# Projections with stationary weights in a four-layer hybrid model: the two halves of the activations side by side under one weight

## The chip, the cores and the metric

The kernel runs on one core of one Trainium2 chip. The metric is the device time of one execution, in microseconds (us), lower is better. Three runs of the kernel before took 2116.32, 2118.42 and 2120.05 us; their median, 2118.42, is the time before.

## What is computed

Four layers on h of 256 tokens by 2048 features, float32 throughout, each followed by a residual and a layer norm. Cut to what the change touches, the projections:

```python
def ssd_mixer(h, ...):                       # layer 0
    z, xbc, dt = split(h @ w_in, [4096, 4096 + 6144])
    xbc = silu(causal_depthwise_conv(xbc, conv_w, conv_b))
    dt = softplus(dt + dt_bias)              # 64 heads
    ...                                      # chunked scan, y
    return (rms_norm_by_group(y * silu(z)) * norm_w) @ w_out
def fox_mixer(h, ...):                       # layer 1
    q, k, v, z, f = split(h @ w_in, ...)     # 16 heads of 128
    cum = cumsum(log_sigmoid(f + f_bias))    # added to the logits
    return (causal_attention(q, k, v, cum) * silu(z)) @ w_out
def mla_mixer(h, ...):                       # layer 2
    q_lat, kv_lat, k_pe, z = split(h @ w_in, ...)
    ...
    return (o * silu(z)) @ w_out
def s5_mixer(h, ...):                        # layer 3
    u, z = split(h @ w_in, 2)
    ...                                      # a scan over time: y
    y = gelu(y)
    y = y * sigmoid(y @ w_glu + b_glu)
    return (y * silu(z)) @ w_out
for i in range(4):
    h = layer_norm(8 ** 0.25 * h + mixer[i](h, ...))
```

## The kernel before

**Every product is three matmuls.** A float32 operand is split in two of type fp32r: a high part (a cast) and a low part (the operand less the cast). `mm3` (L110) issues high weights by high activations (L113), then two cross products (L114, L115), all added in PSUM; low by low is left out. The weights arrive in float32: `half` (L91) loads half a strip, 512 KB, by a DMA that SP issues into `raw` (7 buffers); ACT casts it to `whi` (L102) and VectorE (DVE) subtracts to give `wlo` (L107; 4 buffers each; a share goes to GpSimd, POOL). The activations h are kept transposed, features on partitions: `new_hT` and the layer's end (`out_layer`) write them as 16 blocks `hh` (high) and 16 blocks `hl` (low) of 128x256, four blocks to a tile.

**Three shapes of projection** use them:

- `proj_tok` (PSUM tiles `pt`): the activations are the stationary operand (128x128), 512 columns of weights stream past. SSD's z, all output projections, FoX's v and S5's u are made so.
- `proj_Tk` (`pk`): part of MLA.
- `proj_T` (L134, through `proj_T_steps`, L123): the weights are the stationary operand, and the 256 tokens of hT stream past. One call makes one tile of 128 features by 256 tokens, from 16 blocks (kb) of three matmuls with 256 columns each, in half a bank of PSUM. There are 146 such tiles: 48 of SSD's convolution (`cps`, L471) and one of dt (`dps`); 16 each of FoX's q, k and z (`fox_q`, `fox_k`, `zps`) and one of f (`fps`); 16 of MLA's z, 16 of S5's z (`zps`) and 16 of S5's gate (`gps`). That is 2304 blocks in the 144 wide ones. ACT and DVE read the finished tile from PSUM, several times for most: in SSD ACT scales it and DVE adds three shifted products of it.

**The order.** The program names the work in a written order; `defer(n, f)` puts a piece off by n ticks, and a tick passes with each half strip that a projection uses up. Pieces that wait for another engine are put off so. The scheduler of the language then fixes the order on each engine; each engine works its own row of instructions off in that order and waits where an operand is not there.

**SSD**, eight groups: z (`pt`), then `decay` (POOL broadcasts rows across partitions, L514; DVE subtracts; ACT exponentiates), six convolution tiles, and by ticks `turn_x` (transposes `xp`), `inputs` (POOL scales `xdd` and `xs`, L565), `within` (`yd`; POOL's `gate`, L570), `across` (L595, and the second gate), and `turn_y` (transposes `ypt`, L613, of the `xs` that ACT scaled in L601). So POOL goes from broadcasts to two-input operations and back several times a group.

**FoX**, sixteen heads: `fox_q`, `fox_k`, ACT's copies of both to SBUF (L697), then by ticks the logits (`lps`, L704 and L706; DVE scales and masks them, L708 and L710), the softmax, and `zps`. Between the heads run pieces of S5's parameters (`s5_params`): a transpose `wp` (L1036), POOL's operations `wn` (L1101) to `pn` (L1108), and the store of `pn` from an earlier round, `P_d` (L1053), which ACT's queue issues, so ACT stands at it until `pn` is written.

**S5**: `z_tile` is called between the pieces of the scan; `far` are the matmuls that read the scan's state X. After `gelu`, `gps` tiles use a block order of their own.

Of the kernel before, what the change touches and what calls it, by code (L numbers as in the profile page):

```python
# [19 lines left out]
P = 128  # L20
T = 256
# [9 lines left out]
class Core:  # L31
# [59 lines left out]
    def half(self, src, i, n=2048, spare=None):  # L91
# [6 lines left out]
        if spare:  # L98
            hi, lo = (pool.tile([P, n // 2], F32R, tag=t, bufs=b, name=f"w_{t}") for pool, t, b in spare)
        else:  # L100
            hi, lo = (self.wp.tile([P, n // 2], F32R, tag=t, bufs=4, name=t) for t in ("whi", "wlo"))
# [21 lines left out]
    def proj_T_steps(self, src, hT, ps, m=P, order=range(KB)):  # L123

        for i in range(2):
            w = self.half(src, i, KB * m)
            for j in range(8):
                kb = 8 * i + j
                self.mm3(ps, [x[:, j * m:(j + 1) * m] for x in w], [x[order[kb]] for x in hT], kb == 0, kb == KB - 1)
                if j == 7:  # L130
                    self.tick()
                yield

    def proj_T(self, src, hT, ps, m=P, order=range(KB)):  # L134
        for _ in self.proj_T_steps(src, hT, ps, m, order):
            pass

    def proj_tok(self, srcs, aT, n=512, before=None, tail=None, spare=None):
# [10 lines left out]
        while h < N:  # L149
# [9 lines left out]
            for r, (i, t) in enumerate(runs):  # L159
# [4 lines left out]
                for j in range(2):  # L164
                    for tt in range(2) if t is None else (t,):
                        kb = 2 * (h + i) + j
                        a = [x[kb][:, tt * P:(tt + 1) * P] for x in aT]
# [8 lines left out]
    def proj_Tk(self, srcs, aT):  # L176
# [4 lines left out]
        for q, src in enumerate(srcs):  # L181
            for i in range(2):
                w = self.half(src, i)
                for j in range(2):
                    kb = 4 * q + 2 * i + j
                    a = [x[kb] for x in aT]
# [86 lines left out]
    def out_layer(self, li, parts, gb_tiles, spare, out=None):  # L273
# [10 lines left out]
        hT = ([None] * KB, [None] * KB)  # L284
# [38 lines left out]
        def turn(t, k0, nk):  # L323
            c = k0 // 4
            if t == 0 and k0 % 4 == 0:
                for i, n in enumerate("hl"):
                    x = self.hp.tile([P, 4, T], F32R, tag=f"h{n}{c}", name=f"h{n}{c}")
                    hT[i][4 * c:4 * c + 4] = [x[:, k] for k in range(4)]
                    tiles[i].append(x)
# [4 lines left out]
            hi, lo = (x[c][:, k0 % 4:k0 % 4 + nk, t * P:(t + 1) * P] for x in tiles)  # L334
# [3 lines left out]
        tiles = ([], [])  # L338
# [93 lines left out]
def ssd(C, hT, out):  # L432
# [3 lines left out]
    with C.tc.tile_pool(name="ssd", bufs=1) as sp, C.tc.tile_pool(name="ssd_c", bufs=1) as vp, C.tc.tile_pool(name="ssd_t", bufs=1) as tp:  # L436
# [45 lines left out]
        def decays():  # L482
            dps = C.acc("dps")
            C.proj_T(A["ssd_dt"], hT, dps[0:NH, 0:T], m=NH)
            x = arena[0:NH, 0:T]
            nc.vector.tensor_scalar(x, dps[0:NH, 0:T], dtb, None, op0=ALU.add)
# [137 lines left out]
        for g in range(G):  # L624
# [3 lines left out]
                           [[(C.hp, f"h{n}{c}", 1) for n in "hl"] for c in range(4)], out)  # L628


def fox(C, hT, out):
# [3 lines left out]
    with pool(name="fox", bufs=1) as fp, pool(name="fox_t", bufs=2) as tp, \  # L635
# [13 lines left out]
        fps = C.acc("fps")  # L649
        C.proj_T(A["fox_f"], hT, fps[0:H, 0:T], m=H)  # L650
        x, lf, one = V[2][0:H, 0, 0:T], V[2][0:H, 0, T:], V[2][0:H, 1, 0:T]
        nc.vector.tensor_scalar(x, fps[0:H, 0:T], fb, None, op0=ALU.add)
# [33 lines left out]
        def head(h):  # L686
# [6 lines left out]
            for nm in ("fox_q", "fox_k"):  # L693
                ps = C.acc(nm)
                C.proj_T(A[nm][h], hT, ps[:, 0:T])
                s = tp.tile([P, T], F32, tag=nm, name=nm)
                nc.scalar.copy(s, ps[:, 0:T])  # L697
# [29 lines left out]
            nc.scalar.activation(th, zps[:, 0:T], AF.Tanh, scale=0.5)  # L727
            nc.vector.scalar_tensor_tensor(th, th, 1.0, zps[:, 0:T], op0=ALU.add, op1=ALU.mult)
# [4 lines left out]
        for _ in steps:  # L733
# [3 lines left out]
                           [[(C.hp, f"h{n}{c}", 1) for n in "hl"] for c in range(4)], out)  # L737
# [20 lines left out]
def mla(C, hT, out):  # L758
# [3 lines left out]
    with C.tc.tile_pool(name="mla", bufs=1) as mp, C.tc.tile_pool(name="mla_w", bufs=1) as wp, C.tc.tile_pool(name="mla_t", bufs=2) as tp:  # L762
# [84 lines left out]
        for h in range(H):  # L847
            zps = C.acc("zps")
            C.proj_T(A["mla_z"][h], hT, zps[:, 0:T])
            th = tp.tile([P, T], F32, tag="th", name="th")  # L850
            nc.scalar.activation(th, zps[:, 0:T], AF.Tanh, scale=0.5)
# [653 lines left out]
```

## Time and profile before

| what | value |
|---|---|
| median of 3 runs | 2118.42 us |
| the profiled execution as a whole | 2125.38 us |
| its span, to which all rows refer | 2123.2 us |
| mean clock granted to TensorE | 0.979 of full |
| matmuls in the profile | 14409 |
| read from HBM | 357.81 MB, 175 GB/s with the writes |
| weight casts L102 | 611, 630.3 us of ACT |
| low parts L107 | 610, 763.9 us of DVE |

How to read the rows that the prediction quotes. A row of the timeline is: time from the start of the span, duration, engine, line, operation, output<-inputs, shape, count; in brackets the idle time ahead of it and what ended it ("issue": nothing that the profile shows). A row of the stretches is: from:to and its length, then for each of PE, PEld, DVE, ACT and POOL the busy time with the number of instructions, the granted clock, the mean busy share of the DMA engines and GB/s. The sum and mean row is over all stretches asked for. A row of the waits is: who waits at which line <- whom it waits for, with the sum of the waiting in us, how often, and the longest. A group's row gives the engine, the line, the operation and its tiles, with count and durations in ns (lowest, middle, highest, or busy time and mean). PE is TensorE, PEld its weight load.

### The profile page before, as it was taken

How to read it: one execution, taken by the hardware profiler on the slowest of the kernel's cores; microseconds unless marked ns; L12 is line 12 of the kernel's file. 1: busy time of each engine (PE TensorE's matmuls, PEld its weight loads, DVE VectorE, ACT ScalarE, POOL GpSimd, SP SyncE). 2: the span in 40 equal slices, each digit the busy share in tenths (PEclk: the TensorE clock that was granted, in tenths of full speed). 3: DMA queues.
4: the chain of work that ended last, by engine and by line, in shares of the span. 5: the costliest groups of instructions: out<-in, count | busy, mean ns of one | idle time of the engine just before them, and what ended most of it. 6: DMA issues, size and time to landing. Idle time of an engine off the chain costs nothing.

```text
span 2123.2 us, 36603 instructions
## 1 busy us (share of the span) xinstructions
PE 2030.1 (96%) x14409; PEld 1839.9 (87%) x14409; DVE 1377.3 (65%) x2390; ACT 952.9 (45%) x1434; POOL 393.2 (19%) x477
## 2 busy tenths in 40 slices
PE   8999999999999997899999999999999998989997
PEld 7889988998878876799999978998887898989985
DVE  7777677777754694465655567646556776976655
ACT  5455544455443432344444444545544344345442
POOL 0221222122200017778770000000000000000003
PEclk9999999999999998999999999999999999989999
DMA  8445444544576545565666564654347555576662
GB/s 285 152 150 174 157 140 155 170 149 154 164 233 188 185 141 168 172 205 179 220 186 211 178 207 128 205 181 143 106 149 218 179 178 164 169 222 216 190 188 92
DMA packets 131436, 374.30 MB, mean 176 GB/s; under 512 B 33648, under 2 KB 38208, under 8 KB 130496
## 3 DMA queue, kind: packets, MB, share of 16 engines
q1 hardware_dynamic: 108832, 362.07, 54.1%
q10 hardware_dynamic: 21408, 9.83, 1.6%
q8 instruction: 113, 1.85, 0.4%
q14 instruction: 59, 0.48, 0.1%
q0 software_dynamic: 1024, 0.07, 0.0%
HBM read 357.81 MB, written 14.04 MB: 175 GB/s over the span
## 4 chain that ended last, share of the span: by engine, by line
PE 77%; DVE 11%; DMA 5%; POOL 3%; issue 3%; ACT 2%; SPq 0%; ACTq 0%; DVEq 0%; POOLq 0%
PE pt L115 10%; PE pt L113 10%; PE pt L114 10%; PE cps L115 4%; PE cps L114 4%; PE cps L113 4%; PE zps L113 3%; PE zps L114 3%; PE zps L115 3%; DVE wlo L107 3%; PE fox_q L113 1%; PE gps L113 1%; PE gps L114 1%; PE gps L115 1%; PE fox_k L113 1%
## 5 line engine op out<-in xcount | busy, mean ns | idle before, releaser
L107 DVE TENSOR_TENSOR wlo<-raw,whi 128x1024 fp32r<-128x1024 f32 (+3 forms) x610 | 763.9, 1256 | 510.8 <-ACT whi L102 499.4
L102 ACT CAST whi<-raw 128x1024 fp32r<-128x1024 f32 (+3 forms) x611 | 630.3, 1036 | 834.9 <-PE pt L115 306.5
L113 PE MATMUL pt<-whi,hh 128*128 128x512 f32 (+2 forms) x716 | 283.0, 396 | 17.9 <-ACT whi L102 17.6
L114 PE MATMUL pt<-wlo,hh 128*128 128x512 f32 (+2 forms) x716 | 280.0, 391 | 5.8 <-DVE wlo L107 3.1
L115 PE MATMUL pt<-whi,hl 128*128 128x512 f32 (+2 forms) x716 | 280.8, 392 | 0.4 <-DVE hl L336 0.4
L113 PE MATMUL zps<-hh,whi 128*128 128x256 f32 x768 | 223.3, 291 | 0.0
L115 PE MATMUL zps<-hh,wlo 128*128 128x256 f32 x768 | 220.5, 287 | 0.3 <-DVE wlo L107 0.3
L114 PE MATMUL zps<-hl,whi 128*128 128x256 f32 x768 | 220.5, 287 | 0.0
L114 PE MATMUL cps<-hl,whi 128*128 128x256 f32 x768 | 217.8, 284 | 0.0
L115 PE MATMUL cps<-hh,wlo 128*128 128x256 f32 x768 | 217.8, 284 | 0.0
L113 PE MATMUL cps<-hh,whi 128*128 128x256 f32 x768 | 217.7, 283 | 0.0
L113 PEld LDWEIGHTS pt<-whi,hh 128*128 128x128 f32 x716 | 136.9, 191 | 46.5 <-ACT whi L102 18.4
L114 PEld LDWEIGHTS pt<-wlo,hh 128*128 128x128 f32 x716 | 137.0, 191 | 34.8 <-DVE wlo L107 5.4
L115 PEld LDWEIGHTS pt<-whi,hl 128*128 128x128 f32 x716 | 137.1, 191 | 27.1 <-issue 1.7
L113 PEld LDWEIGHTS zps<-hh,whi 128*128 128x128 f32 x768 | 150.5, 196 | 0.5
L115 PEld LDWEIGHTS zps<-hh,wlo 128*128 128x128 f32 x768 | 150.4, 196 | 0.5 <-DVE wlo L107 0.5
L114 PEld LDWEIGHTS zps<-hl,whi 128*128 128x128 f32 x768 | 150.5, 196 | 0.0
L114 PEld LDWEIGHTS cps<-hl,whi 128*128 128x128 f32 x768 | 147.5, 192 | 0.3
L113 PEld LDWEIGHTS cps<-hh,whi 128*128 128x128 f32 x768 | 147.5, 192 | 0.3
L115 PEld LDWEIGHTS cps<-hh,wlo 128*128 128x128 f32 x768 | 147.5, 192 | 0.1
L113 PE MATMUL pt<-whi,yh 128*128 128x512 f32 x240 | 95.6, 398 | 0.0
L114 PE MATMUL pt<-wlo,yh 128*128 128x512 f32 x240 | 95.5, 398 | 0.0
(503 smaller groups left out, 4253.5 us busy)
## 6 DMA issues: line engine op xcount, KB each, us to landing
raw<-in_ssd_z SPq DMA_DIRECT2D x64, 512.0 KB
raw<-in_ssd_x SPq DMA_DIRECT2D x64, 512.0 KB
raw<-in_ssd_o SPq DMA_DIRECT2D x64, 512.0 KB
raw<-in_fox_v SPq DMA_DIRECT2D x32, 512.0 KB
raw<-in_fox_q SPq DMA_DIRECT2D x32, 512.0 KB
raw<-in_fox_k SPq DMA_DIRECT2D x32, 512.0 KB
raw<-in_fox_z SPq DMA_DIRECT2D x32, 512.0 KB
raw<-in_fox_o SPq DMA_DIRECT2D x32, 512.0 KB
```

Source lines behind the costliest of these rows:

```text
L102: nc.scalar.copy(hi, r)
L107: (nc.gpsimd if on_pool else nc.vector).tensor_tensor(lo, r, hi, op=ALU.subtract)
L113: mm(ps, s[0], m[0], start=first, stop=False)
L114: mm(ps, s[0], m[1], start=False, stop=False)
L115: mm(ps, s[1], m[0], start=False, stop=last)
```

## The change

The high and the low activations of a block come to lie in one tile, `[128, 2, 4, 256]`, so that one access pattern takes both: hT gets a third list, the pair. In `proj_T_steps` a block is now two matmuls, the high weights by the pair (512 columns: high in the tile's first half, low in its second) and the low weights by the high activations (256 columns, added to the first half). A tile of output now fills a bank of PSUM, `[m, 2, 256]`, and the sum of its halves is made by `total`: ACT copies the second half to SBUF, and DVE adds the first to it. Everything behind reads the sum from SBUF. In FoX the copies of q and k were there before; the additions are new. Elsewhere copy and addition are both new, with a new tile `u` in SSD and `z` in FoX.

`proj_tok` and `proj_Tk` take the first two lists and issue what they did. S5's tiles `ux` and `un` become one joint tile `xu` (its gelu output too), and the lists of spare weight buffers name the joint tiles.

```diff
 def half(self, src, i, n=2048, spare=None):
...
+                both = pool.tile([P, 2, n // 2], F32R, tag=t, bufs=b, name=f"w_{t}")
+                hi, lo = both[:, 0], both[:, 1]
...
 def proj_T_steps(self, src, hT, ps, m=P, order=range(KB)):
+        mm = self.nc.tensor.matmul
         for i in range(2):
             w = self.half(src, i, KB * m)
             for j in range(8):
                 kb = 8 * i + j
-                self.mm3(ps, [x[:, j * m:(j + 1) * m] for x in w], [x[order[kb]] for x in hT], kb == 0, kb == KB - 1)
+                hi, lo = (x[:, j * m:(j + 1) * m] for x in w)
+                mm(ps, hi, hT[2][order[kb]], start=kb == 0, stop=False)
+                mm(ps[:, 0], lo, hT[0][order[kb]], start=False, stop=kb == KB - 1)
...
-    def proj_T(self, src, hT, ps, m=P, order=range(KB)):
-        for _ in self.proj_T_steps(src, hT, ps, m, order):
+    def proj_T(self, src, hT, name, m=P):
+        ps = self.acc(name)[0:m].rearrange("p (n t) -> p n t", n=2)
+        for _ in self.proj_T_steps(src, hT, ps, m):
             pass
+        return ps
+
+    def total(self, out, ps):
+        self.nc.scalar.copy(out, ps[:, 1])
+        self.nc.vector.tensor_tensor(out, ps[:, 0], out, op=ALU.add)
...
     def new_hT(self):
-        tiles = [[self.hp.tile([P, 4, T], F32R, tag=f"h{n}{c}", name=f"h{n}{c}") for c in range(4)] for n in "hl"]
-        return tuple([x[k // 4][:, k % 4] for k in range(KB)] for x in tiles)
+        tiles = [self.hp.tile([P, 2, 4, T], F32R, tag=f"h{c}", name=f"h{c}") for c in range(4)]
+        return tuple([tiles[k // 4][:, i, k % 4] for k in range(KB)] for i in (0, 1, slice(0, 2)))
...
         def conv(src, ti, pool_tag, bufs):
-            ps = C.acc("cps")
-            C.proj_T(src, hT, ps[:, 0:T])
+            ps = C.proj_T(src, hT, "cps")
+            u = vp.tile([P, T], F32, tag="u", name="u", bufs=2)
+            C.total(u, ps)
             c = vp.tile([P, T], F32, tag="conv", name="conv", bufs=2)
-            nc.scalar.activation(c, ps[:, 0:T], AF.Identity, bias=cb[:, ti:ti + 1], scale=cw[:, ti, 3:4])
+            nc.scalar.activation(c, u, AF.Identity, bias=cb[:, ti:ti + 1], scale=cw[:, ti, 3:4])
             for k in range(1, 4):
-                nc.vector.scalar_tensor_tensor(c[:, k:], ps[:, 0:T - k], cw[:, ti, 3 - k:4 - k], c[:, k:], op0=ALU.mult, op1=ALU.add)
+                nc.vector.scalar_tensor_tensor(c[:, k:], u[:, 0:T - k], cw[:, ti, 3 - k:4 - k], c[:, k:], op0=ALU.mult, op1=ALU.add)
...
             for nm in ("fox_q", "fox_k"):
-                ps = C.acc(nm)
-                C.proj_T(A[nm][h], hT, ps[:, 0:T])
+                ps = C.proj_T(A[nm][h], hT, nm)
                 s = tp.tile([P, T], F32, tag=nm, name=nm)
-                nc.scalar.copy(s, ps[:, 0:T])
+                C.total(s, ps)
                 qk.append(s)
...
-            zps = C.acc("zps")
-            C.proj_T(A["fox_z"][h], hT, zps[:, 0:T])
+            zps = C.proj_T(A["fox_z"][h], hT, "zps")
+            z = tp.tile([P, T], F32, tag="z", name="z", bufs=1)
+            C.total(z, zps)
...
         def z_tile(kb):
-            zps = C.acc("zps")
-            C.proj_T(A["s5_z"][kb], hT, zps[:, 0:T])
+            C.total(zs[kb], C.proj_T(A["s5_z"][kb], hT, "zps"))
...
         for kb in range(KB):
-            gps = C.acc("gps")
-            C.proj_T(A["s5_glu"][kb], (yh, yl), gps[:, 0:T], order=order)
+            gps = C.acc("gps").rearrange("p (n t) -> p n t", n=2)
+            for _ in C.proj_T_steps(A["s5_glu"][kb], (yh, yl, yb), gps, order=order):
+                pass
             s = tp.tile([P, T], F32, tag="th", name="sg", bufs=3)
-            nc.scalar.activation(s, gps[:, 0:T], AF.Tanh, bias=bg[:, kb:kb + 1], scale=0.5)
+            C.total(s, gps)
+            nc.scalar.activation(s, s, AF.Tanh, bias=bg[:, kb:kb + 1], scale=0.5)
```

The change also moves instructions. In FoX, DVE's row of one head before, from the first low part of a weight half to the two logits operations:

```order
L107 TENSOR_TENSOR wlo<-raw,whi 128x1024
L271 TENSOR_TENSOR y_9665<-yf,y_9664 128x256
L107 TENSOR_TENSOR wlo<-raw,whi 128x1024 x2
L708 SCALAR_TENSOR_TENSOR lg<-lps,ckm 128x256
L710 SCALAR_TENSOR_TENSOR lg<-lps,ck 128x128
```

and the same place now (L153 is the addition in `total`, L112 the low part):

```order
L153 TENSOR_TENSOR fox_q<-fox_q 128x256
L112 TENSOR_TENSOR wlo<-raw,whi 128x1024
L288 TENSOR_TENSOR y_8770<-yf,y_8769 128x256
L112 TENSOR_TENSOR wlo<-raw,whi 128x1024 x2
L153 TENSOR_TENSOR fox_k<-fox_k 128x256
L725 SCALAR_TENSOR_TENSOR lg<-lps,ckm 128x256
L727 SCALAR_TENSOR_TENSOR lg<-lps,ck 128x128
```

The addition of q stands ahead of the three low parts, that of k behind all of them, directly ahead of the logits.

ACT's row of the same head before, from the store of `pn` to the copy of k:

```order
L1053 DMA P_d<-pn 128x8x64
L102 CAST whi<-raw 128x1024
L697 COPY fox_q<-fox_q 128x256
L270 CAST y_9664<-yf 128x256
L102 CAST whi<-raw 128x1024 x2
L697 COPY fox_k<-fox_k 128x256
```

and now (L152 is the copy in `total`, L107 the cast):

```order
L1070 DMA P_d<-pn 128x8x64
L152 COPY fox_q<-fox_q 128x256
L107 CAST whi<-raw 128x1024
L287 CAST y_8769<-yf 128x256
L107 CAST whi<-raw 128x1024 x2
L152 COPY fox_k<-fox_k 128x256
```

The copy of q has moved ahead of the first cast; the rest of the row stands as it did.

In SSD a group's next z (`pt`) fills the gaps between the transposes, in an order set by ticks. TensorE's row before, at the last transposes `xp` of group 0 (`hh_78` is the second tile of high blocks, `hl_82` of low ones):

```order
L113 MATMUL pt_929<-whi,hh_78 128x512
L114 MATMUL pt_929<-wlo,hh_78 128x512
L552 MATMUL xp_774<-ident,xc 128x128
L552 MATMUL xp_775<-ident,xc 128x128
L115 MATMUL pt_929<-whi,hl_82 128x512
```

and now (`h_79` is the third joint tile, L118 to L120 are `mm3`):

```order
L120 MATMUL pt_833<-whi,h_79 128x512
L118 MATMUL pt_832<-whi,h_79 128x512
L570 MATMUL xp_701<-ident,xc 128x128
L570 MATMUL xp_702<-ident,xc 128x128
L119 MATMUL pt_832<-wlo,h_79 128x512
L120 MATMUL pt_832<-whi,h_79 128x512
```

35 `pt` of group 1's z stood between group 0's last convolution matmul and these transposes, 61 stand there now; and behind the last `ypt` of group 7, 657 `pt` of the output projection were left before, 585 now.

More of the change, by code (lines that the diff above doesn't have):

```diff
@@ L98, in half @@
         if spare:
-            hi, lo = (pool.tile([P, n // 2], F32R, tag=t, bufs=b, name=f"w_{t}") for pool, t, b in spare)
+            if len(spare) == 1:
+                (pool, t, b), = spare
+                both = pool.tile([P, 2, n // 2], F32R, tag=t, bufs=b, name=f"w_{t}")
+                hi, lo = both[:, 0], both[:, 1]
+            else:
+                hi, lo = (pool.tile([P, n // 2], F32R, tag=t, bufs=b, name=f"w_{t}") for pool, t, b in spare)
         else:
@@ L283, in out_layer @@
         gb, mean, nm, rs = [None] * 8, [None] * 2, [None] * 2, [None] * 2
-        hT = ([None] * KB, [None] * KB)
+        hT = tuple([None] * KB for _ in range(3))
         def resid(t, cb, ps):
@@ L325, in turn @@
             if t == 0 and k0 % 4 == 0:
[L326 to L329, printed above, removed]
+                x = self.hp.tile([P, 2, 4, T], F32R, tag=f"h{c}", name=f"h{c}")
+                for i, n in enumerate((0, 1, slice(0, 2))):
+                    hT[i][4 * c:4 * c + 4] = [x[:, n, k] for k in range(4)]
+                tiles.append(x)
             pt = self.aux("ptr")
@@ L333, in turn @@
             src = pt[:, 0:nk * P].rearrange("p (a b) -> p a b", a=nk)
-            hi, lo = (x[c][:, k0 % 4:k0 % 4 + nk, t * P:(t + 1) * P] for x in tiles)
+            hi, lo = (tiles[c][:, i, k0 % 4:k0 % 4 + nk, t * P:(t + 1) * P] for i in range(2))
             nc.scalar.copy(hi, src)
             V.tensor_tensor(lo, src, hi, op=ALU.subtract)
-        tiles = ([], [])
+        tiles = []
         def load_gb(k):
@@ L1293, in z_tile @@
         def z_tile(kb):
[L1294 to L1295 removed]
+            C.total(zs[kb], C.proj_T(A["s5_z"][kb], hT, "zps"))
             th = tp.tile([P, T], F32, tag="th", name="th", bufs=3)
[L1297 to L1300 removed]
+            nc.scalar.activation(th, zs[kb], AF.Tanh, scale=0.5)
+            nc.vector.scalar_tensor_tensor(zs[kb], th, 1.0, zs[kb], op0=ALU.add, op1=ALU.mult)
+        yh, yl, yb = ([None] * KB for _ in range(3))
         ys, ready = {}, []
```

50 lines of the change are left out of this document (23 added, 27 removed).

## The prediction

> **What bounds the kernel now.** I read the page first: what TensorE does and what the chain that ended last is made of.
>
> ```profile
> PE 2030.1 (96%) x14409; PEld 1839.9 (87%) x14409; DVE 1377.3 (65%) x2390; ACT 952.9 (45%) x1434; POOL 393.2 (19%) x477
> PE 77%; DVE 11%; DMA 5%; POOL 3%; issue 3%; ACT 2%; SPq 0%; ACTq 0%; DVEq 0%; POOLq 0%
> ```
>
> TensorE looks like the bound, so cheaper matmuls look like time. That is an average over stages, and a busy TensorE is not one at its peak; so next comes its timeline, for the step from one matmul to the next. First and last row of three unbroken stretches: ten steps of 256 columns, fifteen of 512 in the SSD layer, 44 of 512 in its output projection.
>
> ```profile
> 204.76 0.28 PE L115 MATMUL cps<-hh,wlo 128*128 128x256 f32 x1
> 205.96 0.40 PE L113 MATMUL pt<-whi,hh 128*128 128x512 f32 x1
> 300.33 0.39 PE L113 MATMUL pt<-whi,hh 128*128 128x512 f32 x1
> 303.77 0.39 PE L113 MATMUL pt<-whi,hh 128*128 128x512 f32 x1
> 619.69 0.40 PE L113 MATMUL pt<-whi,yh 128*128 128x512 f32 x1
> 629.96 0.40 PE L115 MATMUL pt<-whi,yl 128*128 128x512 f32 x1
> ```
>
> Steps: 1.20/10 = 0.120 us, 3.44/15 = 0.229 us, 10.27/44 = 0.233 us. The time goes with the columns; a matmul has only a small fixed part.
>
> Then I asked stage by stage who is really late. In the SSD layer it is POOL. Its timeline in one group, the cycles of its first operation (L565) from group 0 to group 7 as stretches (the second cycle and the sum of the seven), and what TensorE waits for there:
>
> ```profile
> 170.53 1.82 POOL L570 TENSOR_TENSOR xs<-xs,arena 128x512 f32<-128x512 f32 x1 [6.80 <-issue]
> 178.65 1.57 POOL L514 PARTITION_BROADCAST arena<-rows  x1 [6.29 <-issue]
> 187.97 1.37 POOL L595 TENSOR_TENSOR xs<-xs,off 128x512 f32<-128x512 f32 x1 [7.75 <-issue]
> 195.42 0.80 POOL L514 PARTITION_BROADCAST arena<-rows  x1 [6.08 <-issue]
> 203.27 1.28 POOL L570 TENSOR_TENSOR xs<-xs,arena 128x512 f32<-128x512 f32 x1 [7.05 <-PE cps L115]
> 211.50 0.81 POOL L514 PARTITION_BROADCAST arena<-rows  x1 [6.95 <-issue]
> ...
> 152.93:222.30 69.37, 67.53 (x459) 61.31 (x458) 52.66 (x87) 35.74 (x51) 14.74 (x14) 1.00 0.52 164
> sum 486.41, PE 467.86 PEld 426.26 DVE 349.04 ACT 245.13 POOL 100.60; mean PE 66.84 PEld 60.89 DVE 49.86 ACT 35.02 POOL 14.37
> ...
> PE ypt L613 <- ACT xs L601: 18.5, 7, 3.5
> ```
>
> POOL is busy 14.4 us of a cycle of 486.41/7 = 69.5, yet each change between broadcast and two-input operation costs it 6 to 8 us, mostly put down to nothing. Eight changes make the cycle. TensorE (66.8 busy) waits for it at ypt, 2.6 us a group. **Cheaper matmuls alone cannot shorten these cycles.**
>
> In the FoX layer a second loop runs. One head, by POOL, ACT, DVE and TensorE:
>
> ```profile
> ACT whi L102 <- POOL pn L1108: 77.5, 12, 11.5
> ...
> 985.55 0.87 POOL L1108 TENSOR_TENSOR pn<-t,t 128x320 f32<-128x320 f32 x1
> 996.16 0.73 POOL L1101 TENSOR_TENSOR wn<-t,t 128x256 f32<-128x256 f32 x1 [2.10 <-PE wp L1036]
> ...
> 986.45 0.40 ACTq L1053 DMA_DIRECT2D P_d<-pn  x1
> 986.95 1.05 ACT L102 CAST whi<-raw 128x1024 fp32r<-128x1024 f32 x1 [6.04 <-POOL pn L1108]
> 987.90 0.36 ACT L697 COPY fox_q<-fox_q 128x256 f32<-128x256 f32 x1
> 988.16 0.41 ACT L270 CAST y<-yf 128x256 fp32r<-128x256 f32 x1
> 988.47 1.99 ACT L102 CAST whi<-raw 128x1024 fp32r<-128x1024 f32 x2
> 990.37 0.37 ACT L697 COPY fox_k<-fox_k 128x256 f32<-128x256 f32 x1
> 1006.80 0.40 ACTq L1053 DMA_DIRECT2D P_d<-pn  x1
> ...
> 988.02 1.23 DVE L107 TENSOR_TENSOR wlo<-raw,whi 128x1024 fp32r<-128x1024 f32 x1 [4.15 <-ACT whi L102]
> 989.64 3.26 DVE L107 TENSOR_TENSOR wlo<-raw,whi 128x1024 fp32r<-128x1024 f32 x2
> 992.82 0.42 DVE L708 SCALAR_TENSOR_TENSOR lg<-lps,ckm 128x256 f32<-128x256 f32 x1
> ...
> 991.88 0.38 PE L704 MATMUL lps<-fox_k,fox_q 128*128 128x128 f32 x2
> 995.41 0.60 PE L1036 MATMUL wp<-ident,wn 128*128 128x128 f32 x4
> 1012.21 0.38 PE L704 MATMUL lps<-fox_k,fox_q 128*128 128x128 f32 x2
> ```
>
> Read it round: lps at 991.88, wp at 995.41 after the rest of zps; that frees POOL's wn (996.16); POOL ends in pn; ACT's queue stands until pn is there to issue P_d (1006.80), 12 times; only then come the casts and the copies of q and k. Copy k ends at 990.74, 1.14 before lps, so here TensorE's own order (20.33 a head) still decides, with 1.14 us to spare. But two wlo run on DVE until 992.90.
>
> **The change part by part.** A kb block (three matmuls of 256, 0.360 us) becomes one of 512 and one of 256: 0.349 with the SSD step, 0.353 with the output projection's, so 11 or 7 ns saved. The moving operand now has two pieces 4 KB apart in a partition, which no row shows; if it costs as two matmuls of 256, nothing is saved. I take 11 ns (the SSD rows read the same hT) and keep 0. A tile has 16 blocks: 0.18 us.
>
> The Trainium skill, "TensorE: Matmul & The Clock Gate", section "Back-to-back issue gap", gives N/2.4 + 2.5 ns, which would leave 2.5 ns to save in a block. The rows show 120 and 229 where that gives 109 and 216; here the fixed part is larger, and by the page the sum below would be some 5 us higher.
>
> Added to each of 146 tiles are an ACT copy and a DVE add of 128x256, priced by the nearest rows:
>
> ```profile
> L697 ACT COPY fox_q<-fox_q x16: 363/365/372, 873.0 to 1184.1; 128x256 f32<-128x256 f32 x16
> L708 DVE SCALAR_TENSOR_TENSOR lg<-lps,ckm 128x256 f32<-128x256 f32 x16 | 6.7, 422 | 7.1 <-PE lps L706 7.0
> ```
>
> Some 0.37 and 0.42 us; in FoX q and k the copy was there already. What counts is what stands around them.
>
> *MLA z and S5 glu.* 16 tiles each, TensorE is the bound:
>
> ```profile
> 1352.00:1447.00 95.00, 95.00 (x752) 92.88 (x751) 51.14 (x66) 40.42 (x53) 0.00 (x0) 1.00 0.59 178
> 1931.00:2032.00 101.00, 100.84 (x795) 98.69 (x795) 67.33 (x103) 49.51 (x73) 0.00 (x0) 1.00 0.64 197
> ```
>
> DVE has 44 and 34 us free for 16 adds (6.7): hidden. 2 x 256 x 0.011 = **-5.6**.
>
> *FoX.* The order of DVE puts the add of k behind both wlo. ACT's sum from P_d to the end of copy k is unchanged (copy q only comes ahead of its cast, which shifts the first wlo by 0.36). So: wlo end at about 993.2 (992.90 and most of the shift), add to 993.65, lps at 993.75: 7.3 after P_d instead of 5.43. From lps to the next P_d were 14.92, now 0.09 less for eight blocks of zps. The loop is then 14.83 + 7.3 = 22.1 instead of 20.33: **TensorE, which would need 0.53 less, waits, and a head is 1.8 longer.** It holds for the 12 heads with a P_d in ACT's way: +21.6. In the last four copy and add end about when TensorE arrives: 0.53 saved less 0.2, -1.3. Together **+20**; between -8.4 (16 x 0.53, if the add finds DVE free) and +24 (2 us a head).
>
> *SSD.* POOL's row of operations is the same; its cycles stay at 69.5. Two things move. The first L565 needs the last xp of group 0, and 26 more pt stand ahead of it: 26 x 0.229 less 96 blocks x 0.011 = +4.9. And behind the last ypt 585 pt are left where 657 were: 72 matmuls of the output projection have moved into the cycles, 72 x 0.233 = -16.8. There is room: 10 per cycle are 2.4 us, TensorE has 69.5 - 66.8 + 1.06 (96 blocks) = 3.7. DVE gets 2.5 of adds and 1.3 for one more wlo on 49.9: no bound. **-12**; at the ends -17 (no late start) and +5 (late start alone).
>
> *S5 z.* Scan and splits fill DVE before the scan ends:
>
> ```profile
> 1810.00:1840.00 30.00, 30.00 (x252) 30.00 (x251) 29.67 (x40) 11.95 (x16) 0.00 (x0) 1.00 0.48 146
> ```
>
> About eight adds fall before its end: 8 x 0.42 = 3.4, which TensorE waits for at far; **+4** with a little behind it, from -2.8 (all hidden) to +6.7 (all 16 exposed).
>
> The larger joint tiles (h, y, weight spares) hold the same buffers with the same last readers: nothing, or at most one wait at a layer's start.
>
> Sum: 20 - 5.6 - 12 + 4 = **+6.4 us**. Against the profiled execution (2125.4 with what lies around its span) 2131.8; that execution is 7 above the median of the runs, 2118.4, so I say **2125**.
>
> **The rivals.** *TensorE stays the bound in FoX (faster).* DVE could take the add of k sooner, if the two wlo ran at 1.23 like the first instead of 1.63, or P_d came earlier. For it: 1.14 us of slack; against: the order, and wlo ending 1.02 after lps already. It decides once the add ends before eight blocks of zps have run. Then -8.4 - 5.6 - 12 + 4 = -22: 2096.
>
> *SSD gives nothing back.* POOL starts 5 late and TensorE, starved of casts while ACT stands for POOL's gate, cannot do the extra pt: 20 - 5.6 + 5 + 4 = +23: 2142. Against it: the 3.7 us of room.
>
> *The change doesn't save what it says.* The two-piece stream costs two steps of 120: 20 - 12 + 4 and a little for the last heads, +13: 2131.
>
> **How the numbers follow.** Forecast 0.48, by itself 2114 to 2136; FoX bound by TensorE 0.27; SSD without return 0.17; no saving in the stream 0.08. Cases of both signs count, so the range runs from the second to near the third: 2096 to 2140. A measurement of this kernel tells 0.2% (4.2 us) from no change: faster than 2114 takes the second case and a little of the first, 0.31; within 0.2%, 0.21; slower 0.48.
>
> **What would show it.** lps waiting 1.5 to 2 us for DVE's add in twelve heads, and heads 22 us apart; if they are 19.8 apart, the second case holds. L565 cycles still at 69.5, first one 5 late, no more waits at ypt worth counting but 72 pt fewer after the last. Steps of 0.229 and 0.120 in zps and gps. A far that waits some 3 us longer for X. Wrong it would be if the 512-column step is over 0.24, or if POOL's gaps change.

## The result, and the profile after

The changed kernel takes 2143.44 us (median of 4 runs, 2139.60 to 2149.18) where the kernel before takes 2117.37 beside it: a ratio of 1.0103, 95% interval 1.0075 to 1.0132. A second measurement gave 2142.17 against 2118.88, 1.0114 (1.0090 to 1.0138). So it is slower by 1%, as forecast in sign; the forecast of 2125 was too low, and the median lies 3 above the range's upper end of 2140.

The page of the changed kernel, engines and chain:

```profile
PE 2019.0 (94%) x12073; PEld 1712.5 (80%) x12073; DVE 1438.0 (67%) x2536; ACT 988.7 (46%) x1548; POOL 378.3 (18%) x477
PE 67%; DVE 13%; POOL 7%; DMA 5%; issue 4%; ACT 3%; ACTq 0%; SPq 0%; DVEq 0%; POOLq 0%
```

2336 matmuls fewer, 11 us less busy TensorE, and a span of 2137.8 instead of 2123.2. TensorE's share of the chain has fallen from 77% to 67%, that of DVE and POOL risen from 14% to 20%: TensorE now waits for them. The view of waits says where (waiter, line <- releaser: total us, times, longest):

```profile
PE lps L721 <- DVE fox_k L153: 30.4, 12, 11.3
PE pt L118 <- ACT whi L107: 15.6, 4, 6.4
PE ypt L631 <- ACT xs L619: 12.5, 6, 3.6
PE zps L140 <- DVE wlo L112: 5.8, 7, 2.5
PE ptr L349 <- DVE hres L336: 5.5, 2, 2.8
```

In the kernel before, the row of `lps` was `PE lps L704 <- ACT fox_k L697: 9.3, 1, 9.3`. One head, by POOL, ACT, DVE and TensorE, as the prediction read it:

```profile
1004.60 0.87 POOL L1125 TENSOR_TENSOR pn<-t,t 128x320 f32<-128x320 f32 x1
...
1005.50 0.39 ACTq L1070 DMA_DIRECT2D P_d<-pn  x1
1005.94 0.37 ACT L152 COPY fox_q<-fox_q 128x256 f32<-128x256 f32 x1 [6.01 <-POOL pn L1125]
1006.20 1.05 ACT L107 CAST whi<-raw 128x1024 fp32r<-128x1024 f32 x1
...
1007.46 2.00 ACT L107 CAST whi<-raw 128x1024 fp32r<-128x1024 f32 x2
1009.36 0.37 ACT L152 COPY fox_k<-fox_k 128x256 f32<-128x256 f32 x1
...
1009.32 2.81 DVE L112 TENSOR_TENSOR wlo<-raw,whi 128x1024 fp32r<-128x1024 f32 x2
1012.05 0.41 DVE L153 TENSOR_TENSOR fox_k<-fox_k 128x256 f32<-128x256 f32 x1
...
1012.60 0.46 PE L721 MATMUL lps<-fox_k,fox_q 128*128 128x128 f32 x2 [1.74 <-DVE fox_k L153]
```

POOL ends `pn`, ACT may issue P_d, casts and copies follow, two low parts run on DVE, then the addition of k, 2.3 us behind the copy's end, and only then `lps`: 7.10 us after P_d's issue, where the prediction had 7.3 and the kernel before 5.43.

Because one trace is one execution, each kernel was traced twice (the second traces are the first runs told below). The table cuts the span at the same instructions in all four; `ptr` are the transposes of the layer norm at a layer's end. A last `ptr` or `gps` counts by its end, a first one by its start. In us:

| stretch | before | after | difference of means | predicted |
|---|---|---|---|---|
| start to the last `ptr` of SSD | 763.2, 758.6 | 749.6, 749.5 | -11.3 | -12 |
| to the last `ptr` of FoX | 541.2, 540.3 | 562.4, 564.8 | +22.8 | +20 |
| to the first `ptr` at MLA's end | 357.2, 355.0 | 352.4, 352.6 | -3.6 | -2.8 |
| to MLA's last `ptr` | 20.4, 20.4 | 24.8, 24.6 | +4.3 | 0 |
| to the unbroken run of `gps` | 247.0, 245.2 | 253.7, 254.7 | +8.1 | +4 |
| `gps` | 91.9, 91.8 | 89.1, 88.3 | -3.2 | -2.8 |
| to the end | 102.4, 102.0 | 106.0, 105.0 | +3.3 | 0 |
| **sum** | 2123.2, 2113.3 | 2137.8, 2139.5 | **+20.4** | **+6.4** |

Three terms came out as predicted, and four others carry what is missing. The medians lie 26 and 23 us apart in the two measurements; the traces account for 20 of that, and the rest lies in executions that were not traced.

### The profile page after: what moved, and what is told of

Same layout as the page of the kernel before. It is cut to its first block, busy times and chain, and to the rows that moved or that the text cites. A ratio compares the mean times of both kernels' runs of the same rounds, so it can differ in the third digit from the quotient of the medians.

```text
span 2137.8 us, 32137 instructions
## 1 busy us (share of the span) xinstructions
PE 2019.0 (94%) x12073; PEld 1712.5 (80%) x12073; DVE 1438.0 (67%) x2536; ACT 988.7 (46%) x1548; POOL 378.3 (18%) x477
## 4 chain that ended last, share of the span: by engine, by line
PE 67%; DVE 13%; POOL 7%; DMA 5%; issue 4%; ACT 3%; ACTq 0%; SPq 0%; DVEq 0%; POOLq 0%
PE pt L119 10%; PE pt L120 10%; PE pt L118 10%; PE cps L139 8%; PE zps L139 5%; DVE wlo L112 5%; PE cps L140 4%; PE gps L139 3%; PE zps L140 2%; ACT whi L107 2%; DMA raw<-in_s_z 2%; PE gps L140 1%; PE yd L596 1%; PE pk L208 1%; POOL t L1120 1%
## 5 line engine op out<-in xcount | busy, mean ns | idle before, releaser
L112 DVE TENSOR_TENSOR wlo<-raw,whi 128x1024 fp32r<-128x1024 f32 (+3 forms) x610 | 762.8, 1254 | 417.5 <-ACT whi L107 414.4
L107 ACT CAST whi<-raw 128x1024 fp32r<-128x1024 f32 (+3 forms) x611 | 630.4, 1037 | 655.5 <-PE pt L120 282.5
L118 PE MATMUL pt<-whi,h 128*128 128x512 f32 (+2 forms) x716 | 279.7, 391 | 15.9 <-ACT whi L107 15.6
L139 PE MATMUL zps<-h,whi 128*128 128x512 f32 x768 | 284.0, 410 | 3.3 <-ACT whi L107 3.3
L119 PE MATMUL pt<-wlo,h 128*128 128x512 f32 (+2 forms) x716 | 278.6, 389 | 7.1 <-DVE wlo L112 4.0
L120 PE MATMUL pt<-whi,h 128*128 128x512 f32 (+2 forms) x716 | 278.7, 389 | 0.4 <-DVE h L353 0.3
L139 PE MATMUL cps<-h,whi 128*128 128x512 f32 x768 | 273.9, 400 | 0.0
L140 PE MATMUL zps<-h,wlo 128*128 128x256 f32 x768 | 220.8, 287 | 5.8 <-DVE wlo L112 5.8
L140 PE MATMUL cps<-h,wlo 128*128 128x256 f32 x768 | 217.0, 283 | 0.0
L139 PEld LDWEIGHTS zps<-h,whi 128*128 128x128 f32 x768 | 149.6, 195 | 37.3 <-ACT whi L107 3.5
L118 PEld LDWEIGHTS pt<-whi,h 128*128 128x128 f32 x716 | 136.3, 191 | 43.7 <-ACT whi L107 16.8
L120 PEld LDWEIGHTS pt<-whi,h 128*128 128x128 f32 x716 | 136.5, 191 | 26.5 <-DVE h L353 1.1
L140 PEld LDWEIGHTS zps<-h,wlo 128*128 128x128 f32 x768 | 150.5, 196 | 8.6 <-DVE wlo L112 8.5
L140 PEld LDWEIGHTS cps<-h,wlo 128*128 128x128 f32 x768 | 145.2, 189 | 2.3 <-issue 1.9
L118 PE MATMUL pt<-whi,yh 128*128 128x512 f32 x240 | 95.6, 399 | 0.0
L120 PE MATMUL pt<-whi,yl 128*128 128x512 f32 x240 | 94.9, 397 | 0.0
L139 PE MATMUL fox_k<-h,whi 128*128 128x512 f32 x256 | 91.8, 402 | 0.0
```

What stands on the lines that cost most here:

```text
L107: nc.scalar.copy(hi, r)
L112: (nc.gpsimd if on_pool else nc.vector).tensor_tensor(lo, r, hi, op=ALU.subtract)
L118: mm(ps, s[0], m[0], start=first, stop=False)
L119: mm(ps, s[0], m[1], start=False, stop=False)
L120: mm(ps, s[1], m[0], start=False, stop=last)
L139: mm(ps, hi, hT[2][order[kb]], start=kb == 0, stop=False)
```

## Experiments

Every kernel was timed beside the kernel before on the same chip.

**1. The changed kernel and the kernel before once more**, for second traces.

> The changed kernel once more, unchanged, for a second trace of it and a better ratio to before. Theory A (the FoX loop through ACT's store of pn and DVE's addition of k sets the heads): heads of FoX at 21.9 us without a half-clock window and about 1.55 more with one, as in the first trace; what differs between executions is the number of heads that catch such a window. Theory B (something else varies): the heads read as in the first trace, three windows among them, and the time differs elsewhere. Ratio to before 1.008 to 1.013.

> The kernel before once more, unchanged, for a second trace of it: the first trace was of an execution at 2125.4, above all timed ones. If the surplus lies in one stage, that stage is shorter here: SSD by up to 6 us if POOL's cycles vary (in four traces of the changed kernel's SSD layer its last ypt ended between 590 and 596), or the S5 scan if half-clock windows fall otherwise. FoX heads at 20.33 in any case.

The second execution of the kernel before took 2115.5 instead of 2125.4. It is 4.6 shorter by the end of SSD, 3 more by that of MLA, 2 more in S5; the heads stand at 20.33 in both. In SSD, then, executions of one kernel differ by some 5 us, and a comparison of two single traces would have put +14.6 on the change where the pairs give +20. A half-clock window is a stretch of 3.41 us, or a multiple, in which the granted clock is 0.5 (told further below). In the changed kernel's second trace four of the twelve heads have one, in the first three: Theory A holds for the heads. But one window more or less is 1.55 us, and the executions lie between 2133 and 2152, so something else varies too. Its two traces don't show what; experiment 5 has a candidate.

**2. FoX's q and k as before the change** (`proj_T3` is the old `proj_T`, three matmuls of 256 columns).

```diff
-                ps = C.proj_T(A[nm][h], hT, nm)
+                ps = C.proj_T3(A[nm][h], hT, nm)      # mm3 over the first two lists of hT
                 s = tp.tile([P, T], F32, tag=nm, name=nm)
-                C.total(s, ps)
+                nc.scalar.copy(s, ps)
```

> The changed kernel with FoX's q and k as three matmuls of 256 columns and one copy, as before the change; everything else changed. Theory A: the addition of k is gone from the loop, TensorE sets the heads again, at 20.33 less 0.18 for z: from the first to the twelfth logits 11 x 20.15 = 222 us where the changed kernel had 248.5, no wait at lps for DVE, no half-clock windows there; the last four heads lose 1.4; together 25 us faster than the changed kernel, 2118, ratio to before 1.000. Theory B (the addition of k matters little, the new copy and addition of z or a shortage of casts slow the heads): at most 10 us faster than the changed kernel, 2133 or more.

2121.75 us, ratio 1.0022 (1.0000 to 1.0045): 20 us back by the medians. This median lies between two groups of executions (experiment 5); the trace, of the lower group, has a span of 2114.8, 23 and 25 less than the changed kernel's two. In it the heads step at 20.23, TensorE waits nowhere in them, and from the first to the twelfth logits it takes 224.9 us (222 expected). FoX's loss comes with the two additions, as Theory A has it, and in the waits above it is that of k which ends TensorE's wait; the new copy and addition of z cost nothing that can be seen. The 0.10 a head that z saves (20.33 to 20.23) is 6 ns a block instead of the 11 taken.

**3. The store of `pn` issued by POOL**, in the changed kernel and in the kernel before.

```diff
-        nc.scalar.dma_start(C.P_d[ft, :, gh], pns.pop(n)[...
+        nc.gpsimd.dma_start(C.P_d[ft, :, gh], pns.pop(n)[...
```

> The changed kernel with the store of pn (P_d) issued by POOL's queue, which writes pn, instead of ACT's; the additions stay. Theory A: ACT no longer stands until pn is there, casts and copies come as they are called for, DVE's addition of k ends ahead of TensorE's eighth block of zps: heads at 20.33 - 0.53 = 19.8, from the first to the twelfth logits 218 where the changed kernel had 248.5, so 30 us faster, 2113, ratio to before 0.998. Theory B (the addition of k behind two low parts is late by itself, whatever ACT waits for): heads stay at 21.9 or more. Theory C: issuing costs POOL so much that its own row becomes the loop: heads of 21 to 24 us.

> The kernel before with the store of pn issued by POOL's queue, nothing else. Theory A (in the kernel before, TensorE itself sets the heads and ACT's standing is covered by 1.1 us of slack): heads stay at 20.33; only the single wait of 9.3 at the first logits can go, against some 8 us that the second and third head cost where POOL issues: 2110 to 2120, ratio 0.996 to 1.001. Theory B (moving the store helps any kernel, and the gain of 35 us over the changed kernel had little to do with the additions): 2085 to 2095.

The changed kernel with this edit takes 2106.62, ratio 0.9962 (0.9934 to 0.9990): faster than both kernels, 36 less than the changed one (34 and 36 by the spans of the traces). The additions are all still there. One head of it:

```profile
987.94 0.88 POOL L1125 TENSOR_TENSOR pn<-t,t 128x320 f32<-128x320 f32 x1
...
990.25 0.93 POOL L1070 DMA_DIRECT2D P_d<-pn  x1
...
987.14 1.05 ACT L107 CAST whi<-raw 128x1024 fp32r<-128x1024 f32 x1 [1.80 <-PE fox_k L139]
990.26 1.05 ACT L107 CAST whi<-raw 128x1024 fp32r<-128x1024 f32 x1 [2.06 <-PE fox_k L140]
991.21 0.37 ACT L152 COPY fox_k<-fox_k 128x256 f32<-128x256 f32 x1
...
992.55 0.41 DVE L153 TENSOR_TENSOR fox_k<-fox_k 128x256 f32<-128x256 f32 x1
...
993.11 0.35 PE L721 MATMUL lps<-fox_k,fox_q 128*128 128x128 f32 x1 [0.34 <-DVE fox_k L153]
```

ACT now casts one strip at a time, as TensorE frees a buffer (`<-PE fox_k`), so the low parts no longer queue in a pair ahead of the addition. The steady heads take 20.1 to 20.4, so Theory B falls; C too, though the second and third logits come 26.6 and 21.7 after the one before them, and from the first to the twelfth it takes 230.0, not the expected 218. The expected 19.8 isn't reached even where TensorE waits for nothing: such heads step at 20.06 to 20.24, so their 48 blocks save at most 0.27 and not 0.53. The wait for the addition, in the head shown 0.34, is the longest of the steady heads.

In the kernel before the same edit gives 2107.44, ratio 0.9943 (0.9924 to 0.9961), 11 us: the steady heads have nothing to gain, but from the first `fps` matmul to the first logits it takes 99.0 where it took 116.9 and 116.1, against 8.9 lost right behind. That is faster than Theory A's 2110 to 2120 and far from Theory B's 2085 to 2095. So of the 36 us, some 11 come from the edit in the kernel before too, and 25 are what the additions cost when they stand in the loop through ACT's queue. The traces of the FoX layer say 28: it is 36 and 39 shorter than in the changed kernel's two, and 9 and 8 in the kernel before.

**4. S5's z as before the change; an early place for S5's spare strip.**

```diff
-            C.total(zs[kb], C.proj_T(A["s5_z"][kb], hT, "zps"))
+            zps = C.proj_T3(A["s5_z"][kb], hT, "zps")   # read from PSUM by ACT and DVE
...
-    spare=[((sp, "xu3", 1),), ((wp, "sc", 2), (wp, "sc", 2))]
+    spare=[((wp, "ys", 1), (wp, "ut", 1)), ((wp, "sc", 2), (wp, "sc", 2))]
```

> The changed kernel with S5's z as three matmuls of 256 columns, read from PSUM as before; everything else changed. Theory A (the additions of z fall among DVE's work for the scan and delay what far waits for): from S5's first transposes to the last yp 6.8 us lost in the changed kernel, of which 4 to 7 come back: 2137 to 2139. Theory B (the stage differs for the joint tile xu or by half-clock windows): no change within 2 us, 2142 to 2145.

> The changed kernel with the store of pn issued by POOL, S5's z as three matmuls of 256 read from PSUM, and the spare weight strip of S5's u in two tiles that are free early instead of the joint tile. Theory A: to the kernel with POOL's store alone (2106.6) it gains 4 at the end of the third layer (the cast of that strip stands ahead of the last transposes again) and 5 in S5's scan: 2098, ratio 0.990. Theory B (those stages differ by chance of the half-clock windows): 2105 to 2108.

The first edit alone: 2139.99, ratio 1.0112 (1.0082 to 1.0143), against 1.0114 without it; the times can't tell 2 us. The trace can: from MLA's last `ptr` to the run of `gps` it takes 248.0 where the changed kernel took 253.7 and 254.7, and the kernel before 247.0 and 245.2. Over all traces, the four with the changed z take 250.6 to 254.7 there and the ten with the old z 244.7 to 249.2. All three edits together: 2104.07, ratio 0.9921 (0.9893 to 0.9950). There that stretch takes 245.3, and the one ahead of it 20.4 again instead of 24.8. Theory A has both gains in the trace. The expected 9 us doesn't show in the medians, 2104.07 against 2106.62; the spread of experiment 5 covers it. ACT's casts at the end of MLA show the second one (kernel before; changed kernel; all three edits):

```profile
1643.00 1.05 ACT L102 CAST w_un<-raw 128x1024 fp32r<-128x1024 f32 x1 [5.16 <-DMA raw<-in_s_u]
1644.26 1.05 ACT L102 CAST w_sc<-raw 128x1024 fp32r<-128x1024 f32 x1 [0.21 <-DMA raw<-in_s_u]
1662.24 1.25 ACT L335 CAST hh<-ptr 128x512 fp32r<-128x512 f32 x2 [5.22 <-PE ptr L332]
```

```profile
1649.37 1.05 ACT L107 CAST w_sc<-raw 128x1024 fp32r<-128x1024 f32 x1 [7.22 <-DMA raw<-in_s_u]
1665.02 1.25 ACT L352 CAST h<-ptr 128x512 fp32r<-128x512 f32 x2 [5.20 <-PE ptr L349]
...
1679.32 1.05 ACT L107 CAST w_xu<-raw 128x1024 fp32r<-128x1024 f32 x1
```

```profile
1633.39 1.05 ACT L107 CAST w_ys<-raw 128x1024 fp32r<-128x1024 f32 x1 [6.62 <-DMA raw<-in_s_u]
1635.99 1.05 ACT L107 CAST w_sc<-raw 128x1024 fp32r<-128x1024 f32 x1 [1.55 <-DMA raw<-in_s_u]
1649.94 1.25 ACT L368 CAST h<-ptr 128x512 fp32r<-128x512 f32 x2 [5.52 <-PE ptr L365]
```

A strip of S5's u has its high part cast ahead of the layer norm's last transposes in the first and third kernel, so that TensorE has work between those transposes. In the changed kernel it goes to the joint tile `xu3`, in another pool than `un3` was, and its cast has come to stand behind all but the last of ACT's casts of the transposed blocks: the cover of the layer norm is gone. TensorE then waits inside this stretch, where the kernel before loses only 0.2:

```profile
PE ptr L349 <- DVE hres L336: 2.7, 1, 2.7
```

A half-clock window behind this wait makes up the rest of the 4.3. The other traces bear it out: in all nine traces in which the strip goes to `xu3` TensorE waits these 2.7 us and the stretch takes 23.5 to 24.8; in the five in which it goes to `un3`, or to `ys` and `ut`, it takes 20.4. Whether the pool or the tile's other uses moved the cast isn't shown.

**5. The change in SSD alone** (FoX, MLA and S5 with three matmuls of 256 and without sums; the joint tiles stay).

> The change in the SSD layer alone: FoX, MLA and S5 make all their tiles with three matmuls of 256 columns and read them from PSUM as before (the joint tiles of h and S5 stay). Theory A (SSD gains as its z and its output projection move into POOL's cycles, 8 to 14 us by the traces of the changed kernel; the joint spare tile in S5 costs 4): end of the first layer 8 to 14 earlier than before, heads at 20.33, S5's scan as before, 2108 to 2114, ratio 0.995 to 0.998. Theory B (the SSD gain is taken back behind, for the heads or the loads are late anyway): 2116 to 2122.

2127.65, ratio 1.0044 (1.0022 to 1.0066), slower than either theory had it, with two of twelve executions below 2117 and ten from 2124 to 2137; yet the traced one (2116.6) ends SSD at 751.3, 7 to 12 ahead of the kernel before. The other kernels had shown such groups as well: fox_qk_plain six executions from 2113 to 2119 and six from 2125 to 2134, pd_pool seven to 2107 and five above 2118. The kernel before has 41 executions timed beside these kernels, all but two below 2124. The trace of the kernel with three edits had caught an execution of the upper kind. Its output projection in SSD, two stretches of 40 us, and the changed kernel's beside it (us, PE busy (matmuls), PEld, DVE, ACT, POOL, then the granted clock):

```profile
600.00:640.00 40.00, 40.00 (x151) 28.80 (x150) 17.25 (x15) 12.94 (x13) 0.00 (x0) 1.00 0.53 180
640.00:680.00 40.00, 40.00 (x151) 28.80 (x150) 17.18 (x16) 13.36 (x13) 0.00 (x0) 1.00 0.47 162
```

```profile
600.00:640.00 40.00, 40.00 (x173) 32.21 (x172) 20.69 (x20) 14.72 (x14) 0.00 (x0) 1.00 0.63 207
640.00:680.00 40.00, 40.00 (x173) 32.20 (x172) 18.06 (x15) 14.84 (x15) 0.00 (x0) 1.00 0.56 184
```

151 matmuls against 173 in the same time, in the same order, with TensorE never waiting and a granted clock of 1.00 in both: steps of 40/150 = 0.267 us instead of 0.231. From the last `ypt` to the last `ptr` it takes 179 us where the changed kernel takes 158, and the kernel before 176. None of the other thirteen traces has such a stage. That it makes the upper group of the other kernels too is a guess from the size of the gap, as no other execution of an upper group was traced.

**6. Is the long step a pattern that another matmul ends?** One transpose ahead of every 96 matmuls of that stage:

```diff
+            def pause(x):
+                if x in (-8, 0):
+                    tr(C.aux("brk")[:, 0:P], C.ident, C.ident)
+                if before is not None:
+                    before(x)
+            return C.proj_tok([A["ssd_o"][cb, q] for q in range(8)], yT, before=pause, **kw)
```

> The kernel with the change in SSD alone once more, unchanged. Its executions lay between 2110 and 2137, ten of twelve above 2124, while the one in the trace took 2116.6 with 512-column steps of 0.233 in SSD's output projection; in the trace of the kernel with three edits that stage steps at 0.267 instead, from the last ypt to the layer norm's first transposes, and is 20 us longer. Theory S (the spread of the changed kernels is this stage, stepping at 0.267 in one execution and at 0.233 in another): a trace of an execution above 2124 has steps of 0.267 there, one below 2117 has 0.233. Theory T (the spread lies in POOL's cycles or in half-clock windows): steps of 0.233 whatever the time.

> The change in SSD alone, with one transpose of the identity matrix into a spare PSUM bank ahead of every 96 matmuls of SSD's output projection (eight in all; what it writes is not read). Theory S1 (the long step is a pattern in which back-to-back 512-column matmuls lock, and any other matmul ends it, as the transposes at the stage's end did): no stretch stays long for more than 22 us, all executions between 2110 and 2120, median 2115, ratio to before 0.997 to 0.999, at 0.3 us for each transpose. Theory S2 (a limit on the core, such as its supply): the step stays 0.267 in most executions, median 2127 to 2131 as without the transposes.

> The kernel with POOL's store, S5's z of three matmuls and the early spare strip, with the same eight transposes. Its executions fell into 2091 to 2094 and 2104 to 2112. Theory S1: only the lower ones, with 2 us for the transposes: 2093 to 2097, ratio to before 0.989. Theory S2: both, median 2104 to 2107.

> The kernel with the change in SSD alone and the eight transposes once more. In its first job its unbroken twin had no execution with a long stage either (2106 to 2118), so that nothing was told apart there; in another job the twin had ten of twelve. Theory S1 (any other matmul ends the long step): all executions between 2106 and 2122 again. Theory S2 (a limit on the core that a transpose does not lift): where this job has long stages, two groups some 17 us apart, the upper one at 2124 to 2137. A single group at 2106 to 2122 leaves the two undecided.

The unbroken kernel with the change in SSD alone took 2112.13 this time, ratio 0.9974 (0.9956 to 0.9991), ten executions from 2106 to 2118 and none above; its traced one, at 2117.5, steps at 0.233. Theory T expects that as well as Theory S does, so the two stay undecided: a second trace of the long stage is missing. With transposes: 2114.59, 0.9989 (0.9970 to 1.0007), and 2112.80, 0.9985 (0.9970 to 0.9999), 24 executions from 2105.7 to 2122.6. As the unbroken kernel showed no upper group on that chip either, S1 and S2 stay undecided. The kernel with three edits and transposes took 2091.95, ratio 0.9882 (0.9855 to 0.9908), the fastest of all, on the same chip; three of the seven executions without transposes took 2091 to 2094 as well, and whether the transposes have a part in it is open.

## Why the prediction was right or wrong

**Right: the mechanism that decides the sign.** The addition of k behind two low parts, in a loop that runs through POOL's `pn` and ACT's blocked queue, makes TensorE wait in the heads with a P_d. From P_d to `lps` 7.10 (7.3 predicted), heads of 21.9 where nothing else happens (22.1), and the last four heads 0.8 shorter together (1.3). Experiments 2 and 3 took away the addition and the blocked queue, one at a time, and either brought the heads back to 20.1 to 20.4.

**Right: SSD's two movements.** POOL's cycles: L565, now L583, starts its groups from 89.8 to 572.3 where they started from 83.6 to 570.0; seven cycles of 68.9 and 69.5 (69.0 and 68.7 in the second traces), not moved by cheaper matmuls. The first start is 6.2 later, 5.0 in the second traces (4.9 predicted). From the last `ypt` to the last `ptr` (kernel before; changed kernel)

```profile
586.32 0.87 PE L613 MATMUL ypt<-ident,xs 128*128 128x128 f32 x6
...
762.59 0.60 PE L332 MATMUL ptr<-ident,hres 128*128 128x128 f32 x4
```

```profile
590.32 0.88 PE L631 MATMUL ypt<-ident,xs 128*128 128x128 f32 x6
...
749.02 0.60 PE L349 MATMUL ptr<-ident,hres 128*128 128x128 f32 x4
```

it takes 158.4 instead of 176.0, so -17.6 (-16.8 predicted, from 72 `pt` moved into the cycles). Between them the cycles themselves vary: the last `ypt` ends at 582 to 587 in the three traces of kernels with the old SSD layer, at 590 to 598 in eleven with the new. What the prediction had no price for is the long step of experiment 5, which takes the whole gain back in the one trace that has it. That the layer's -11.3 lies so near -12 is in part luck, as its executions differ by some 5 us.

**Right: MLA's z and S5's gate** (-3.6 and -3.2 for -2.8 each; one half-clock window in the first trace of the kernel before is in the former).

**Wrong in size: S5's z, +8.1 for +4.** "About eight adds fall before its end: 8 x 0.42 = 3.4, which TensorE waits for at far" has a wait that came, and leaves a larger one out. TensorE's waits at `far` and at z's own tiles (kernel before; changed kernel):

```profile
PE far L1330 <- ACT ys L1333: 4.4, 2, 2.9
PE far L1330 <- ACT X L1267: 3.9, 1, 3.9
PE far L1330 <- DVE ys L1335: 1.6, 2, 0.8
PE zps L115 <- DVE wlo L107: 0.3, 1, 0.3
```

```profile
PE zps L140 <- DVE wlo L112: 5.8, 7, 2.5
PE far L1347 <- ACT X L1285: 4.7, 1, 4.7
PE far L1347 <- ACT yt L1365: 3.7, 1, 3.7
PE zps L139 <- ACT whi L107: 3.3, 1, 3.3
PE far L1347 <- ACT ys L1350: 1.7, 1, 1.7
PE far L1347 <- DVE ys L1352: 0.8, 1, 0.8
```

At `far` that is 9.9 before and 10.9 after (7.6 and 11.3 in the second traces), +2.4 in the mean. The step that failed is that z's own tiles were given no wait for their weights. They wait 5.8 for low parts, which stand in DVE's queue behind the scan and the additions (0.3 before; 4.6 and 0.1 in the second traces). Four of these seven waits fall while DVE is full (busy for 29.65 of the 30 us from 1817 on), three behind that. Another 3.3 goes to a high part (3.9 in the second trace; none before). The waits for low parts are the mark of the change: 4.2 to 5.8 in the four traces with the changed z, at most 1.0 in the ten without. The high part's wait is not, as the kernel with the change in SSD alone has 3.2 of it. The other waits of this stretch are 3.4 shorter. The upper bound, 6.7 for all 16, was not one, as it counted the additions alone and not the strips behind them.

**Wrong: the joint tiles, +4.3 for "nothing, or at most one wait at a layer's start"** with the price 0. They hold the same buffers for the same readers, but one moved from one pool to another, and a cast moved past the transposes (experiment 4). The order of ACT's casts, available beforehand, shows it; it wasn't read at this place.

**Wrong: waits priced at their own length.** In FoX 1.8 us a head were taken for the wait alone; the eleven steps from the first to the twelfth logits cost 23 more than before, of which (21.9 - 20.33) x 11 = 17. Most of the rest is the half-clock windows that follow such waits:

```profile
989.00:989.70 0.70, 0.66 (x5) 0.69 (x6) 0.00 (x0) 0.00 (x0) 0.00 (x0) 0.83 0.98 328
989.70:993.00 3.30, 3.30 (x13) 2.87 (x13) 2.55 (x7) 0.00 (x1) 0.73 (x1) 0.52 0.78 250
993.00:996.00 3.00, 3.00 (x31) 2.57 (x30) 1.40 (x5) 2.58 (x7) 1.03 (x2) 1.00 0.62 199
...
990.71 0.63 PE L139 MATMUL zps<-h,whi 128*128 128x512 f32 x1
991.13 0.42 PE L140 MATMUL zps<-h,wlo 128*128 128x256 f32 x1
991.35 0.63 PE L139 MATMUL zps<-h,whi 128*128 128x512 f32 x1
```

After a wait of 1.95 us at `lps` the granted clock is about half for 3.41 us: 13 matmuls in 3.3 us, then 31 in 3.0, and a block steps at 0.64 instead of 0.35. It comes in three heads of the first trace and four of the second, and makes such a head 23.6 instead of 21.9. In the last stretch, too, the first trace has such windows of 6.8 us in the middle of the output projection, where those of the kernel before have none; that is 3.4 of its +3.6. In the second trace one window of 3.41 us makes 1.7 of +3.0; the rest stays open.

What decides is the place of the wait on a grid. In each of the fourteen traces all half-clock windows start on one grid of 3.41 us. A full-clock grid window was followed by half clock in every case in which TensorE had been idle for more than 1.95 us of it, and in none with less than 1.55 us (188 were followed, 7941 were not, from 50 us on; idle by the ends that the profile models). A wait of 1.6 to 2.1 us at `lps` lies just there: it brings a window if nearly all of it falls between two grid points.

The Trainium skill, "TensorE: Matmul & The Clock Gate", section "What's actually happening", gives half rate by windows of 3.4 us, which this trace shows, and names an idle window of that length as the cause. Here some 1.55 to 1.95 us of idle time within a window were enough.

The 7 to 11 ns saved in a block were right at their lower end in FoX (6, experiment 2) and about right at the upper in S5's gate (12). So "TensorE, which would need 0.53 less" in a head was twice too much: with POOL's store, heads without a wait step at 20.06 at best, 0.27 less. That lowers what the rival with TensorE as the bound could have won. That the two-piece stream costs more than one of 512 columns is refuted: 0.23 us in `zps` and `cps`.

## What to carry to other kernels

An instruction added behind a PSUM tile is not priced by its duration but by what stands ahead of it in its engine's queue, and by the loop in which that queue stands: find the DMA or wait on which a queue stands still, and move that first; here one DMA issued by another engine was worth 36 us in the changed kernel and 11 in the old. Where a buffer changes its pool, read the order of all that writes it, spare uses too. And trace a kernel more than once: here two executions of one kernel differed by 10 us, as much as half the effect.

## What the runs showed of the hardware that was not expected

- A wait of about 2 us can cost another 1.5: 3.41 us at half clock after it, when TensorE is idle for more than some 1.55 to 1.95 us within one window of a 3.41 us grid.
- In one traced execution the 512-column matmuls of one stage step at 0.267 us instead of 0.233 for 155 us, with no wait, no change of order and a granted clock of 1.00; the step ends with the first transposes behind the stage. Groups of times 15 to 20 us apart, on two of the three chips on record, suggest it in other executions, only in kernels with the new SSD layer. Its cause, and whether the new order brings it on, stay open.
- POOL's change between broadcasts and two-input operations leaves it idle for 5.8 to 8.0 us in SSD where the profile names nothing that ended it (5.8 to 8.8 in the kernel before). Issuing the store of `pn` took 0.93 us of POOL, which made it the better place for a store that POOL's own result feeds.
